# Compressed attention of a two-layer decoder trunk: two token blocks through one chain of small steps, the zeroing factor in the gates, and 8 KB of DMA scratch

## The chip, the cores and the metric

The kernel runs on one core of a Trainium2 chip. The metric is the device time of one execution in microseconds (us), lower is better. A core has a matrix engine (PE, with its weight loads listed apart as PEld), a vector engine (DVE), a scalar engine (ACT), a general engine (POOL) and a queue engine (SP) that only starts transfers. Each engine works through its own instructions in order, and the engines wait for one another through semaphores.

## The reference, cut to what matters

The program computes two decoder layers on 512 tokens of width 1024. Layer 0 holds the part that is changed: sparse attention with three branches, whose outputs are added with sigmoid gates. The first branch is the compressed one. Keys and values are compressed to 31 entries (one per 16 tokens, each covering 32), and each query attends to those that end at or before its own position:

```python
m_c = cmp_end[None, :] <= t[:, None]
p_c = masked_softmax(jnp.einsum('bgrqd,bgcd->bgrqc', q_b, k_c) * scale, m_c)
o_c = jnp.einsum('bgrqc,bgcd->bgrqd', p_c.astype(v_c.dtype), v_c)
o_c = jnp.where(m_c.any(-1)[:, None], o_c, 0)
...
return g_b[..., 0:1] * o_c + g_b[..., 1:2] * o_s + g_b[..., 2:3] * o_w
```

The `where` sets the result to zero for the first 31 tokens, which see no compressed entry at all. The other two branches (selected blocks and a window) are, at 512 tokens, both causal attention over all earlier tokens, with keys and values of their own.

There are 12 query heads in 3 groups of 4; a group shares its keys and values. Beside them layer 0 has attention over a memory of 256 entries. An output projection, a squared-ReLU MLP, and a second layer with its own attention and MLP follow.

## The kernel before, in words

**Stages.** The tokens lie in four blocks of 128. `setup` and the first part of `layer_a` compute the projection of group 0 and of the compressed branch (to about 60 us). Then comes the attention of layer 0 (to about 300 us), the output projection, the MLP of layer 0 (to about 660 us), layer B with its attention (to about 930 us) and the second MLP. The MLPs are long rows of matrix products.

**Items.** `attend` (L142) walks through a list of items. An item has a front (scores, maximum, exponential, scaling) and a back (transposes of the probabilities, their copy out of PSUM, and at the end of a half the product with the values). The back of an item is issued after the front of the next one. A *light* item of the two token branches covers a query block with at most 256 keys and takes one PSUM tile for its scores (L1050); a *heavy* one takes two (L1063). The order within a group is four light items, four heavy ones, and the same again for the second pair of heads.

**Compressed items.** `cmp_scores` (L969) builds the front and back of a compressed item, one per token block and group, 12 in all. The front is four small matrix products (L985) into a PSUM tile, then a chain: two DVE additions that read that tile (L990 with the mask, L991 with its second half), a DVE maximum (L993), a DVE subtraction (L994), an exponential on ACT (L995), a DVE sum (L997), a reciprocal (L998), a multiplication with the gate (L1003; for block 0 L1001, which also multiplies with `self.zc`, the column of zeros for the first 31 tokens), and a multiplication of the probabilities on POOL (L1004). The PSUM tile is free again when L991 has read it. The back is one transpose (L1009) and its copy into `pcT` by `evT` (L737): every third call goes to DVE (L741), the others to ACT (L743), counted by the running number `self.n`, which every new tile raises too. When the last block's back is done, `close` (L1037) runs the product with the compressed values (L1015, in `cmp_out`).

**PSUM tiles for scores.** Three banks serve all score tiles in turn (`ps`, L207, with `pS` and `px`), for the transposes there are two (`pT`).

**Where the items stand.** `spread` (L173) puts the compressed items between the others: in group 0 all four after the eighth item; in groups 1 and 2 one after each of the first four items (L841).

**Filler.** After every front and every back `tick` (L147) takes some steps from a list of other work: the projections of the next group (`proj_a`), of the memory queries (`mem_q`), the memory keys, and more. `RA` (L47) says how many steps per tick in each of the three groups and in the memory items. Two of these jobs start only when 20 items of a group have been issued (`seen.count(...) == 20`, L834 and L835). A second list, `slow`, starts one step of `blocks` (L1172) after every 13 ticks (`PA`): a transfer within device memory of 1 MB, four plain ones from ACT's queue (L1180) and then four that add, from POOL's queue (L1183), for each quarter of each MLP. The MLP goes on with them, eight per quarter (`PM`).

**Order.** The program is written in this order, but a planner in the framework orders each engine's instructions before the run from estimated durations, so an engine's row in the trace need not follow the source.

Of the kernel before, what the change touches and what calls it, by code (L numbers as in the profile page):

```python
# [11 lines left out]
ALU = mybir.AluOpType  # L12
AX = mybir.AxisListType

P = 128
D = 1024
S = 512
NB = 4
# [28 lines left out]
RA = (2.0, 1.16, 1.46, 1.96)  # L47
# [133 lines left out]
class K:  # L181
# [602 lines left out]
    def layer_a(self):  # L784
# [8 lines left out]
        def evac0(b, ps):  # L793
            t = self.t("x", [P, 384])
            nc.scalar.activation(t, ps[:, 0:384], AF.Copy, scale=st[0][:, b : b + 1])
            raw0.append(t)
            nc.scalar.activation(gt[:, b, :], ps[:, 384:420], AF.Copy, scale=st[0][:, b : b + 1])
            if b < NB - 1:
                return
            ga = ab[:, 0:144]  # L800
            nc.vector.tensor_scalar(out=ga, in0=ga, scalar1=-1.0, scalar2=80.0, op0=ALU.mult, op1=ALU.min)
            nc.scalar.activation(ga, ga, AF.Exp)
            nc.vector.tensor_scalar(out=ga, in0=ga, scalar1=1.0, scalar2=None, op0=ALU.add)
            nc.vector.reciprocal(out=ga, in_=ga)

# [28 lines left out]
        work.add(self.proj_a(2, xg, st, ga[2]), "g2", lambda: seen.count(0) == 20)  # L834
        work.add(self.mem_q(0, xg, ins["w_am"], e, qm), None, lambda: seen.count(1) == 20)  # L835
# [5 lines left out]
        items = spread(L[0], C[0], 8, 0) + spread(L[1], C[1], 1, 1) + spread(L[2], C[2], 1, 1) + M  # L841
# [127 lines left out]
    def cmp_scores(self, g, q4, cmp, gt):  # L969
# [12 lines left out]
        def front(i):  # L982
            Sc = self.ps(self.pS, [P, 4, 2, 32])
            for h in range(4):
                nc.tensor.matmul(  # L985
                    Sc[:, h].rearrange("p t c -> p (t c)"), q4[h // 2][:, h % 2, i * P : (i + 1) * P],
                    KC[:, g].rearrange("p t c -> p (t c)"), start=True, stop=True,
                )
            s = self.t("cs", [P, 4, 32])
            nc.vector.tensor_tensor(out=s, in0=Sc[:, :, 0], in1=bcast(self.ccm[:, i, :], 1, 4), op=ALU.add)  # L990
            nc.vector.tensor_tensor(out=s, in0=Sc[:, :, 1], in1=s, op=ALU.add)  # L991
            m = self.t("c1", [P, 4])
            nc.vector.tensor_reduce(out=m, in_=s, axis=AX.X, op=ALU.max)  # L993
            nc.vector.tensor_tensor(out=s, in0=s, in1=bcast(m, 2, 32), op=ALU.subtract)  # L994
            nc.scalar.activation(s, s, AF.Exp)  # L995
            z = self.t("c2", [P, 4])
            nc.vector.tensor_reduce(out=z, in_=s, axis=AX.X, op=ALU.add)  # L997
            nc.vector.reciprocal(out=z, in_=z)  # L998
            gc = gt[:, i, :].rearrange("p (h b) -> p h b", b=3)[:, 4 * g : 4 * g + 4, 0]
            if i == 0:  # L1000
                nc.vector.scalar_tensor_tensor(out=z, in0=z, scalar=self.zc, in1=gc, op0=ALU.mult, op1=ALU.mult)  # L1001
            else:
                nc.vector.tensor_tensor(out=z, in0=z, in1=gc, op=ALU.mult)  # L1003
            nc.gpsimd.tensor_tensor(out=s, in0=s, in1=bcast(z, 2, 32), op=ALU.mult)  # L1004
            return s

        def back(i, s):
            pt = self.ps(self.pT, [P, P])
            nc.tensor.transpose(pt, s.rearrange("p h c -> p (h c)"), self.idf)  # L1009
            self.evT(pcT[:, i * P : (i + 1) * P], pt)  # L1010
# [9 lines left out]
    def attn_a(self, g, ga, gt, cmp, out):  # L1020
# [60 lines left out]
        def back(pr, half, hp, ii, p):  # L1081
# [43 lines left out]
            [Item(cfront, cback, (i,), g, "cmp") for i in range(NB)],  # L1125
# [695 lines left out]
```

## Time and profile before

| what | us |
|---|---|
| median of 3 runs | 1273.14 |
| lowest, highest | 1271.8, 1274.15 |
| the profiled execution, its own time | 1268.89 |
| its span, first to last instruction | 1267.1 |

Busy time over that span: PE 1238.2, PEld 1019.6, DVE 835.9, ACT 750.7, POOL 343.1. The granted clock of the matrix engine was 0.998 over the span. A busy PE means that one of its matrix products is under way; products overlap, so a busy PE need not be at its peak rate.

The views that the next part uses are these. The page begins with the busy time of each engine. A table of stretches gives the busy time of each engine between two times. The list of waits says which engine stood still for whom, at which line. Groups of instructions by line give count, total busy time and mean duration; kept apart by shape they tell how the duration of an operation grows with its size. The timeline lists single instructions, with the idle time before them in square brackets and what ended it.

### The profile page before, as it was taken

Reading aid. Unit: us, or ns where it says so; the run is one execution under the profiler, and the core shown is the slowest. Engines: PE = TensorE matmul, PEld = TensorE weight load, DVE = VectorE, ACT = ScalarE, POOL = GpSimd, SP = SyncE. Lnnn points to the kernel's source line nnn. Section 1 sums busy time; section 2 is a strip of 40 time slices with the busy share of each in tenths; the row PEclk is TensorE's granted clock in tenths of the full one; section 3 lists DMA queues with packets and bytes.
Section 4 is the critical chain, followed back from the end, with each engine's and each line's share of the span. In section 5 each row is a group of like instructions: output and inputs, shape, how many; then the busy total and the mean of one; then the engine's idle time right before and its main releaser. Section 6 shows DMA issues by size and latency. Waiting matters only on the chain.

```text
span 1267.1 us, 18289 instructions
## 1 busy us (share of the span) xinstructions
PE 1238.2 (98%) x6416; PEld 1019.6 (80%) x6416; DVE 835.9 (66%) x1516; ACT 750.7 (59%) x1668; POOL 343.1 (27%) x448
## 2 busy tenths in 40 slices
PE   9999989899999999999999999999999999999998
PEld 7768777677788888888888898987788888888887
DVE  6846676755656557566579567787766756656566
ACT  6845578774575364453647457788666445364462
POOL 4546675632040010000002788552222000000000
PEclk9999999999999999999999999999999999999999
DMA  7531241335488697896976331210459789696534
GB/s 266 198 112 65 68 132 61 67 76 135 157 250 239 225 274 220 268 242 216 282 205 190 120 101 58 63 47 9 117 190 277 220 271 241 219 279 204 164 102 164
DMA packets 61835, 215.26 MB, mean 170 GB/s; under 512 B 6736, under 2 KB 14928, under 8 KB 61232
## 3 DMA queue, kind: packets, MB, share of 16 engines
q1 hardware_dynamic: 50656, 143.69, 34.2%
q0 software_dynamic: 9344, 35.77, 14.2%
q10 hardware_dynamic: 1744, 34.63, 7.6%
q8 instruction: 51, 0.84, 0.3%
q14 instruction: 40, 0.33, 0.1%
HBM read 208.83 MB, written 72.35 MB: 222 GB/s over the span
## 4 chain that ended last, share of the span: by engine, by line
PE 80%; DVE 7%; ACT 7%; POOL 2%; issue 2%; DMA 2%; ACTq 0%; POOLq 0%; DVEq 0%
PE s_ps L270 13%; PE s_ps L271 13%; PE s_ps L272 13%; PE s_acc L270 6%; PE s_acc L271 6%; PE s_acc L272 6%; PE s_po L747 3%; PE s_pt L270 3%; PE s_pt L272 3%; PE s_pt L271 3%; ACT s_p L226 1%; DVE s_w L265 1%; PE s_acc L880 1%; PE s_acc L579 1%; PE s_pt L1100 1%
## 5 line engine op out<-in xcount | busy, mean ns | idle before, releaser
L265 DVE TENSOR_TENSOR s_w<-s_st,s_w 128x1024 fp32r<-128x1024 f32 (+3 forms) x254 | 291.0, 1151 | 260.5 <-ACT s_w L263 250.8
L263 ACT ACTIVATE s_w<-s_st 128x1024 fp32r<-128x1024 f32 (+4 forms) x260 | 251.5, 970 | 182.4 <-PE s_pt L272 45.9
L270 PE MATMUL s_ps<-s_act,s_w 128*128 128x512 f32 x568 | 222.0, 393 | 1.1 <-ACT s_act L305 0.7
L271 PE MATMUL s_ps<-s_act,s_w 128*128 128x512 f32 x568 | 221.1, 390 | 0.0
L272 PE MATMUL s_ps<-s_act,s_w 128*128 128x512 f32 x568 | 221.0, 390 | 0.0
L270 PEld LDWEIGHTS s_ps<-s_act,s_w 128*128 128x128 f32 x568 | 106.5, 188 | 24.4 <-ACT s_act L305 1.6
L271 PEld LDWEIGHTS s_ps<-s_act,s_w 128*128 128x128 f32 x568 | 106.7, 188 | 22.9 <-issue 0.8
L272 PEld LDWEIGHTS s_ps<-s_act,s_w 128*128 128x128 f32 x568 | 106.6, 188 | 22.1
L226 ACT ACTIVATE s_p<-s_ps 128x512 f32<-128x512 f32 x64 | 38.2, 598 | 117.9 <-PE s_ps L272 117.1
L270 PE MATMUL s_acc<-s_w,s_act 128*128 128x512 f32 (+3 forms) x288 | 101.4, 357 | 2.3 <-ACT s_sq L518 1.5
L271 PE MATMUL s_acc<-s_w,s_act 128*128 128x512 f32 (+3 forms) x288 | 101.2, 354 | 0.2 <-DVE s_w L265 0.2
L272 PE MATMUL s_acc<-s_w,s_act 128*128 128x512 f32 (+3 forms) x288 | 100.4, 354 | 0.0
L1183 POOL DMA_DIRECT2D sum<-in_w_db_dram x16 | 14.4, 900 | 291.1 <-ACT s_p L226 287.5
L735 POOL TENSOR_SCALAR s_p<-s_p,s_cr,s_ab 128x128 f32<-128x128 f32 (+3 forms) x96 | 61.1, 673 | 55.3 <-DVE s_cr L1076 28.5
L226 ACT ACTIVATE s_p<-s_ps,s_nm 128x256 f32<-128x256 f32 (+3 forms) x128 | 65.6, 523 | 16.4 <-DVE s_nm L726 5.0
L270 PEld LDWEIGHTS s_acc<-s_w,s_act 128*128 128x128 f32 x288 | 54.7, 190 | 8.7 <-ACT s_sq L518 2.5
L743 ACT ACTIVATE s_pt<-s_pt 128x512 f32<-128x512 f32 (+2 forms) x101 | 53.0, 528 | 13.6 <-PE s_pt L1100 6.0
L305 ACT ACTIVATE s_qk<-s_p 128x256 fp32r<-128x256 f32 (+1 forms) x96 | 46.9, 489 | 21.1 <-DVE s_p L1193 19.2
L271 PEld LDWEIGHTS s_acc<-s_w,s_act 128*128 128x128 f32 x288 | 54.8, 190 | 4.7 <-DVE s_w L265 0.4
L272 PEld LDWEIGHTS s_acc<-s_w,s_act 128*128 128x128 f32 x288 | 54.7, 190 | 4.3
L1183 POOL DMA_DIRECT2D sum<-sum x16 | 14.1, 883 | 151.0 <-issue 39.2
L308 DVE TENSOR_TENSOR s_qk<-s_p,s_qk 128x256 fp32r<-128x256 f32 (+1 forms) x96 | 50.0, 520 | 0.7 <-ACT s_qk L305 0.6
(332 smaller groups left out, 2869.3 us busy)
## 6 DMA issues: line engine op xcount, KB each, us to landing
s_st<-in_w_up_dram SPq DMA_DIRECT2D x64, 512.0 KB, 4.3
s_st<-sum SPq DMA_DIRECT2D x64, 512.0 KB, 6.7
s_st<-in_w_db_dram SPq DMA_DIRECT2D x48, 512.0 KB, 4.5
sum<-in_w_db_dram POOLq DMA_DIRECT2D x16, 1024.0 KB, 14.1
sum<-sum POOLq DMA_DIRECT2D x16, 1024.0 KB, 11.0
s_st<-in_w_bq_dram SPq DMA_DIRECT2D x16, 384.0 KB, 3.1
s_st<-in_w_ag_dram SPq DMA_DIRECT2D x11, 512.0 KB, 3.4
s_w<-in_w_c_dram SPq DMA_DIRECT2D x8, 512.0 KB, 4.4
```

The source lines that it names most:

```text
L226: return lambda *a, **k: self.marks.append(f(*a, **k))
L263: nc.scalar.activation(w[:, 0], st, AF.Copy)
L265: e.tensor_tensor(out=w[:, 1], in0=st, in1=w[:, 0], op=ALU.subtract)
L270: mm(ps, lh[0], rh[0], start=start, stop=False, skip_group_check=again)
L271: mm(ps, lh[0], rh[1], start=False, stop=False, skip_group_check=again)
L272: mm(ps, lh[1], rh[0], start=False, stop=stop, skip_group_check=again)
L305: nc.scalar.activation(dst[:, 0], src, AF.Copy)
L308: nc.vector.tensor_tensor(out=dst[:, 1], in0=src, in1=dst[:, 0], op=ALU.subtract)
L735: self.nc.gpsimd.tensor_scalar(out=p, in0=p, scalar1=c, scalar2=g, op0=ALU.mult, op1=ALU.mult)
L743: self.turned = self.nc.scalar.activation(dst, src, AF.Copy)
L747: i = self.nc.tensor.matmul(*a, **k)
L1183: self.behind(self.nc.gpsimd.dma_start(t[o], x, accum_op=ALU.add, max_dma_last_dim=4096))
```

## The change

A compressed item now takes two token blocks. Its front issues eight matrix products into one PSUM tile of twice the size (one full bank), and every step of the chain works on both blocks at once; its back issues two transposes into one tile, with one copy. There are two items per group, six in all. The factor `zc` is multiplied into the gates of block 0 once, for all 12 heads, in `evac0`, right after the gates have been computed. `RA` is raised in the first three entries in the ratio of the item counts (20 to 18 items per group), the conditions on the item count go from 20 to 18, and in groups 1 and 2 the compressed items stand after the first and the third of the other items (`every` is 2 in place of 1). The scratch for transfers issued by software, a parameter of the program, is set to 8192 bytes.

```diff
-RA = (2.0, 1.16, 1.46, 1.96)
+RA = (2.22, 1.29, 1.62, 1.96)
...
             nc.vector.reciprocal(out=ga, in_=ga)
+            g0 = gt[:, 0, :].rearrange("p (h k) -> p h k", k=3)[:, :, 0]
+            nc.vector.tensor_scalar(out=g0, in0=g0, scalar1=self.zc, scalar2=None, op0=ALU.mult)
...
-        work.add(self.proj_a(2, xg, st, ga[2]), "g2", lambda: seen.count(0) == 20)
-        work.add(self.mem_q(0, xg, ins["w_am"], e, qm), None, lambda: seen.count(1) == 20)
+        work.add(self.proj_a(2, xg, st, ga[2]), "g2", lambda: seen.count(0) == 18)
+        work.add(self.mem_q(0, xg, ins["w_am"], e, qm), None, lambda: seen.count(1) == 18)
...
-        items = spread(L[0], C[0], 8, 0) + spread(L[1], C[1], 1, 1) + spread(L[2], C[2], 1, 1) + M
+        items = spread(L[0], C[0], 8, 0) + spread(L[1], C[1], 1, 2) + spread(L[2], C[2], 1, 2) + M
...
-            Sc = self.ps(self.pS, [P, 4, 2, 32])
-            for h in range(4):
...
+            Sc = self.ps(self.pS, [P, 2, 4, 2, 32])
+            for b in range(2):
+                blk = slice((2 * i + b) * P, (2 * i + b + 1) * P)
+                for h in range(4):
...
-            nc.vector.tensor_tensor(out=s, in0=Sc[:, :, 0], in1=bcast(self.ccm[:, i, :], 1, 4), op=ALU.add)
-            nc.vector.tensor_tensor(out=s, in0=Sc[:, :, 1], in1=s, op=ALU.add)
-            m = self.t("c1", [P, 4])
+            s = self.t("cs", [P, 2, 4, 32])
+            nc.vector.tensor_tensor(out=s, in0=Sc[:, :, :, 0], in1=bcast(self.ccm[:, 2 * i : 2 * i + 2], 2, 4), op=ALU.add)
+            nc.vector.tensor_tensor(out=s, in0=Sc[:, :, :, 1], in1=s, op=ALU.add)
+            m = self.t("c1", [P, 2, 4])
             nc.vector.tensor_reduce(out=m, in_=s, axis=AX.X, op=ALU.max)
...
-            if i == 0:
-                nc.vector.scalar_tensor_tensor(out=z, in0=z, scalar=self.zc, in1=gc, op0=ALU.mult, op1=ALU.mult)
-            else:
-                nc.vector.tensor_tensor(out=z, in0=z, in1=gc, op=ALU.mult)
-            nc.gpsimd.tensor_tensor(out=s, in0=s, in1=bcast(z, 2, 32), op=ALU.mult)
+            nc.vector.tensor_tensor(out=z, in0=z, in1=gc, op=ALU.mult)
+            nc.gpsimd.tensor_tensor(out=s, in0=s, in1=bcast(z, 3, 32), op=ALU.mult)
             return s

         def back(i, s):
-            pt = self.ps(self.pT, [P, P])
-            nc.tensor.transpose(pt, s.rearrange("p h c -> p (h c)"), self.idf)
-            self.evT(pcT[:, i * P : (i + 1) * P], pt)
+            pt = self.ps(self.pT, [P, 2, P])
+            for b in range(2):
+                nc.tensor.transpose(pt[:, b], s[:, b].rearrange("p h c -> p (h c)"), self.idf)
+            self.evT(pcT[:, 2 * i * P : (2 * i + 2) * P].rearrange("p (b q) -> p b q", b=2), pt)
...
-            if i == NB - 1:
+            if i == NB // 2 - 1:
...
-            [Item(cfront, cback, (i,), g, "cmp") for i in range(NB)],
+            [Item(cfront, cback, (i,), g, "cmp") for i in range(NB // 2)],
...
-    nc = bacc.Bacc("TRN2", target_bir_lowering=False, num_devices=1)
+    nc = bacc.Bacc("TRN2", target_bir_lowering=False, num_devices=1, dynamic_dma_scratch_size=8192)
```

More of the change, by code (lines that the diff above doesn't have):

```diff
@@ L982, in front @@
         def front(i):
-            Sc = self.ps(self.pS, [P, 4, 2, 32])
-            for h in range(4):
[L985 to L991, printed above, removed]
@@ L992, in front @@
-            m = self.t("c1", [P, 4])
+            Sc = self.ps(self.pS, [P, 2, 4, 2, 32])
+            for b in range(2):
+                blk = slice((2 * i + b) * P, (2 * i + b + 1) * P)
+                for h in range(4):
+                    nc.tensor.matmul(
+                        Sc[:, b, h].rearrange("p t c -> p (t c)"), q4[h // 2][:, h % 2, blk],
+                        KC[:, g].rearrange("p t c -> p (t c)"), start=True, stop=True,
+                    )
+            s = self.t("cs", [P, 2, 4, 32])
@@ L993, in front @@
+            nc.vector.tensor_tensor(out=s, in0=Sc[:, :, :, 0], in1=bcast(self.ccm[:, 2 * i : 2 * i + 2], 2, 4), op=ALU.add)
+            nc.vector.tensor_tensor(out=s, in0=Sc[:, :, :, 1], in1=s, op=ALU.add)
+            m = self.t("c1", [P, 2, 4])
             nc.vector.tensor_reduce(out=m, in_=s, axis=AX.X, op=ALU.max)
-            nc.vector.tensor_tensor(out=s, in0=s, in1=bcast(m, 2, 32), op=ALU.subtract)
+            nc.vector.tensor_tensor(out=s, in0=s, in1=bcast(m, 3, 32), op=ALU.subtract)
@@ L995, in front @@
             nc.scalar.activation(s, s, AF.Exp)
-            z = self.t("c2", [P, 4])
+            z = self.t("c2", [P, 2, 4])
             nc.vector.tensor_reduce(out=z, in_=s, axis=AX.X, op=ALU.add)
             nc.vector.reciprocal(out=z, in_=z)
-            gc = gt[:, i, :].rearrange("p (h b) -> p h b", b=3)[:, 4 * g : 4 * g + 4, 0]
-            if i == 0:
-                nc.vector.scalar_tensor_tensor(out=z, in0=z, scalar=self.zc, in1=gc, op0=ALU.mult, op1=ALU.mult)
-            else:
-                nc.vector.tensor_tensor(out=z, in0=z, in1=gc, op=ALU.mult)
@@ L1004, in front @@
-            nc.gpsimd.tensor_tensor(out=s, in0=s, in1=bcast(z, 2, 32), op=ALU.mult)
+            gc = gt[:, 2 * i : 2 * i + 2, :].rearrange("p b (h k) -> p b h k", k=3)[:, :, 4 * g : 4 * g + 4, 0]
+            nc.vector.tensor_tensor(out=z, in0=z, in1=gc, op=ALU.mult)
+            nc.gpsimd.tensor_tensor(out=s, in0=s, in1=bcast(z, 3, 32), op=ALU.mult)
             return s
         def back(i, s):
-            pt = self.ps(self.pT, [P, P])
-            nc.tensor.transpose(pt, s.rearrange("p h c -> p (h c)"), self.idf)
```

## The prediction

> **What bounds the kernel now.** I read the busy times of the page first, then busy time by stretch, then the list of waits of the matrix engine in the stretches that hold compressed items, then the timeline there.
>
> ```profile
> PE 1238.2 (98%) x6416; PEld 1019.6 (80%) x6416; DVE 835.9 (66%) x1516; ACT 750.7 (59%) x1668; POOL 343.1 (27%) x448
> ```
>
> PE is busy in all but 28.9 of 1267.1 us. The change removes no matrix product and no transpose: 48 products of L985 and 12 transposes of L1009 stay. So it can only win where PE stands still, and the question is how much of its idle time belongs to the compressed items. The next view is the table of stretches (length, busy time and instructions of each engine). The first two hold the compressed items of groups 1 and 2 from the first product of L985 to the last transpose of L1009; the other three are what lies before, between and behind.
>
> ```profile
> core 0: us, PE busy (x) PEld busy (x) DVE busy (x) ACT busy (x) POOL busy (x), PEclk, DMA share, GB/s
> 168.00:191.00 23.00, 19.81 (x145) 16.09 (x146) 19.30 (x55) 17.64 (x58) 14.48 (x21) 1.00 0.43 139
> 222.00:245.00 23.00, 19.52 (x148) 15.17 (x149) 17.32 (x56) 16.38 (x58) 13.48 (x24) 1.00 0.37 64
> 150.00:168.00 18.00, 16.55 (x107) 13.14 (x105) 13.27 (x27) 13.81 (x36) 14.02 (x17) 1.00 0.20 59
> 191.00:222.00 31.00, 28.54 (x220) 22.98 (x219) 21.06 (x52) 25.82 (x80) 17.04 (x25) 1.00 0.19 60
> 245.00:281.00 36.00, 33.84 (x213) 26.48 (x213) 20.89 (x49) 27.90 (x83) 15.24 (x23) 1.00 0.36 85
> ```
>
> In the first two PE is idle 3.19 + 3.48 = 6.67 of 46 us; in the neighbours 1.45 + 2.46 + 2.16 = 6.07 of 85 us, which is 0.071 per us. At that rate 46 us would have 3.28 us of idle, so 3.39 us are in excess. The engine that differs is DVE: busy 36.62 of 46 us (0.796) with compressed items, 55.22 of 85 (0.650) without. ACT is not busier there (0.740 against 0.795). The waits of PE in the same two stretches (total, times, longest), the three largest of each:
>
> ```profile
> PE s_ps L1065 <- ACT s_p L226: 1.0, 1, 1.0
> PE s_ps L1052 <- DVE s_cs L991: 0.8, 1, 0.8
> PE s_ps L1065 <- DVE s_cs L991: 0.7, 2, 0.4
> ...
> PE s_pt L1100 <- DVE s_pt L741: 1.3, 1, 1.3
> PE s_ps L1065 <- ACT s_p L226: 1.1, 2, 0.9
> PE s_pt L1009 <- ACT s_pt L743: 0.8, 1, 0.8
> ```
>
> PE waits for a score bank that L991 has not yet read (1.5 us), or that an exponential (L226) has not, which itself comes behind a DVE maximum. The 1.3 us go back to the chain too, as the DVE timeline shows:
>
> ```profile
> 226.15 1.43 DVE L994 TENSOR_TENSOR s_cs<-s_cs,s_c 128x128 f32<-128x128 f32 x1
> 227.51 0.54 DVE L741 COPY s_pt<-s_pt 128x384 f32<-128x384 f32 x1
> ...
> 225.50 2.78 POOL L735 TENSOR_SCALAR s_p<-s_p,s_cr,s_ab 128x512 f32<-128x512 f32 x4
> ```
>
> (The last row is POOL's.) The copy that PE waited for stood behind a subtraction of the chain that took 1.43 us. So in these stretches the bound is DVE's queue, and the chain is what fills it.
>
> **The chain, before and after.** These are the chain's groups between 60 and 300 us (count | busy us, mean ns | idle before).
>
> ```profile
> L990 DVE TENSOR_TENSOR s_cs<-s_ps,c 128x128 f32<-128x128 f32 x12 | 3.3, 277 | 2.6 <-PE s_pt L1009 2.0 <-PE s_ps L985 0.5
> L991 DVE TENSOR_TENSOR s_cs<-s_ps,s_cs 128x128 f32<-128x128 f32 x12 | 3.4, 284 | 0.1
> L993 DVE TENSOR_REDUCE s_c<-s_cs 128x4 f32<-128x128 f32 x12 | 3.4, 280 | 0.1
> L994 DVE TENSOR_TENSOR s_cs<-s_cs,s_c 128x128 f32<-128x128 f32 x12 | 4.8, 400 | 0.1
> L997 DVE TENSOR_REDUCE s_c<-s_cs 128x4 f32<-128x128 f32 x12 | 3.3, 277 | 1.1 <-ACT s_cs L995 1.1
> L998 DVE RECIPROCAL s_c<-s_c 128x4 f32<-128x4 f32 x12 | 2.0, 170 | 0.1
> L1001 DVE SCALAR_TENSOR_TENSOR s_c<-s_c,c,s_ab 128x4 f32<-128x4 f32 x3 | 2.3, 780 | 0.0
> L1003 DVE TENSOR_TENSOR s_c<-s_c,s_ab 128x4 f32<-128x4 f32 x9 | 2.8, 309 | 0.2
> L995 ACT ACTIVATE s_cs<-s_cs 128x128 f32<-128x128 f32 x12 | 3.7, 310 | 3.1 <-DVE s_cs L994 3.0
> L1004 POOL TENSOR_TENSOR s_cs<-s_cs,s_c 128x128 f32<-128x128 f32 x12 | 4.8, 400 | 3.0 <-DVE s_c L1003 2.4 <-PE s_ps L1066 0.4 <-DVE s_c L1001 0.2
> ```
>
> DVE spends 25.3 us on 84 instructions. For the doubled size I take other lines that work on 128x256 in the same stretch:
>
> ```profile
> L958 DVE TENSOR_TENSOR s_tq<-s_acc,gr 128x256 f32<-128x256 f32 x8 | 3.3, 418 | 0.7 <-ACT s_x L955 0.6
> L520 DVE TENSOR_REDUCE s_r<-s_sq 128x4 f32<-128x256 f32 x8 | 3.3, 413 | 5.0 <-ACT s_sq L518 5.0
> L711 DVE TENSOR_TENSOR s_qki<-s_tq,s_qki 128x256 fp32r<-128x256 f32 x6 | 3.2, 528 | 0.7 <-ACT s_qki L710 0.5
> L518 ACT ACTIVATE s_sq<-s_acc 128x256 f32<-128x256 f32 x8 | 3.1, 385 | 0.0
> L743 ACT ACTIVATE s_pt<-s_pt 128x256 f32<-128x256 f32 x8 | 3.1, 383 | 0.3 <-PE s_pt L1094 0.3
> L759 POOL TENSOR_TENSOR s_tq<-s_tq,s_r 128x256 f32<-128x256 f32 x4 | 2.5, 618 | 1.2 <-DVE s_r L527 1.2
> L743 ACT ACTIVATE s_x<-s_pt 128x128 f32<-128x128 f32 x8 | 2.2, 276 | 1.9 <-PE s_pt L1009 1.9
> ```
>
> - **DVE:** a pair costs 2 x 0.418 (L990, L991) + 2 x 0.413 (L993, L997) + 0.528 (L994, both inputs in SBUF like L711) + 0.170 + 0.309 = 2.67 us, six pairs 16.0 us. Saved: 9.3 us, or 0.775 per block; for the 8 blocks of the two stretches 6.2 us.
> - **ACT and POOL:** six exponentials of 0.385 in place of 12 of 0.310 save 1.4 us; a copy of 0.383 replaces two of 0.276; six multiplications of 0.618 in place of 12 of 0.400 save 1.1 us. None is the bound; I put these at nothing.
> - **From DVE to PE:** DVE's share falls from 0.796 to (36.62 - 6.2) / 46 = 0.661, which is 0.92 of the way to the neighbours. I take the same part of the excess: 0.92 x 3.39 = 3.1 us. The upper end is all 3.39, or, if the idle time of both stretches went entirely, 6.67. The lower end: only the waits that name the chain or its copies (0.8 + 0.7 + 1.3 + 0.8 = 3.6) come half as often, 1.8 us.
> - **Group 0:** its four blocks lie beside the projection of group 1, and no large wait of PE names them. Nothing; had that filler run out, DVE's 3.1 us there would count too, as a gain.
>
> L994 is blocked, not slow: other instructions of its size take a fifth of its 1.43 us, and POOL was reading SBUF meanwhile (the four scalings of L735 shown above). On this the Trainium skill, SBUF — State Buffer, section Who interferes with whom, says that a DVE instruction with two SBUF inputs and a GpSimd instruction that reads SBUF exclude each other. By that rule half the instructions meet half the collisions, as the means above have it; if collisions grew with the elements instead, DVE would save less, and the gain would lie nearer its lower end.
>
> **The factor in the gates.** One DVE instruction more, on 48 columns, behind the reciprocal of the gates. The nearest row:
>
> ```profile
> L801 DVE TENSOR_SCALAR s_ab<-s_ab x1: 235/235/235, 52.8 to 52.8; 128x144 f32<-128x144 f32 x1
> ```
>
> I charge 0.2 us in full, since PE waits shortly there; the bounds are 0 and 0.235.
>
> **Order and filler.** Per group the ticks give 40 x 2.0 = 80 steps before and 36 x 2.22 = 79.9 after, 46.4 and 46.4, 58.4 and 58.3: the same filler, with its weight loads on SP. In groups 1 and 2 two light items now lie between the compressed ones, and none stands right ahead of the first heavy item. At nothing: PE-bound filler covers it.
>
> **Transfers within device memory.** The items fall from 68 to 62, the ticks from 136 to 124. The 12th item is out after 22 ticks, so 114 become 102, and with one start in 13 ticks after the first 13, eight starts become seven. The eighth, an adding one on POOL, moves into the first eighth of the MLP.
>
> ```profile
> L1183 POOL DMA_DIRECT2D sum<-sum x16: 872/880/923, 253.5 to 1146.4; - x16
> ...
> DMA to landing us min/median/max: 7.7/13.2/17.5
> ```
>
> It takes POOL 0.88 us and lands within 17.5; its sum is needed only in the third product after eight up-projections, each of 24 matrix products. At nothing; if that cover were gone, 13.2 us would show. The scratch of 8 KB also costs nothing in my sum: no issue in the row above stretches (923 ns at most). From the other side, one issue held until an earlier transfer lands would hold POOL's queue, and the scalings of L735 in it, for 13.2 us.
>
> **Sum.** -3.1 + 0.2 = -2.9 us. Against the profiled execution 1268.89 gives 1266.0. The median of the runs shown is 4.25 us above that execution; I carry the difference over: 1273.1 - 2.9 = **1270.2 us**.
>
> **Rivals.**
>
> *A, only the named waits shrink.* The largest single wait in both stretches has ACT's exponential behind it, and ACT is as busy as before. If freeing DVE doesn't move these, the gain is 1.8 - 0.2 = 1.6 us: 1271.5. For it: the 2.1 us of L226. Against it: the maxima that precede these exponentials stand in DVE's queue.
>
> *B, slower: the bank is held longer.* A pair keeps its score bank from its first product until L991 has read both blocks, and PE's next scores wait in order behind that.
>
> ```profile
> 168.73 0.63 PE L985 MATMUL s_ps<-KC,s_qk 128*128 128x64 f32 x4
> 105.99 0.86 PE L985 MATMUL s_ps<-KC,s_qk 128*128 128x64 f32 x7
> 183.34 0.27 PE L1009 MATMUL s_pt<-c,s_cs 128*128 128x128 f32 x1
> ```
>
> Eight products take some 0.95 us for 0.63, the two additions 0.84 for 0.56: 0.60 us more per pair. It decides once PE reaches the next scores before L991 has ended; that was so at 3 of 8 blocks, 0.5 us each. Were it so at all four pairs, PE would lose 4 x 1.1 = 4.4 in place of 1.5 us: +2.9 + 0.2 = +3.1, 1276.2. Against it: the bank falls due half as often, and no longer right ahead of a heavy item. The longer chain itself holds nobody: the first transpose of group 1 came 14.6 us after its scores. The Trainium skill speaks for B: Perfetto Trace Analysis, section Optimizing Scalar/DVE Operations, advises breaking instructions up where an engine that isn't saturated causes bubbles on another; DVE is such an engine here, and the change does the opposite.
>
> *C, the stage is planned anew.* The idle 6.07 us of the neighbours hangs on an order that the planner now makes again, with other items side by side and copies falling otherwise to DVE or ACT. Half of it more or less is 3 us: with the forecast's gain 1267.2 to 1273.2, with none of it up to 1276.
>
> *D, the scratch.* One held issue: POOL 13.2 us late, of which I estimate 10 reach PE beyond the 3 of filler, minus the gain: about 1280. Against it stand the even durations of L1183.
>
> **How the numbers follow.** Chances: forecast (gains of 1.5 to 4.5 us) 0.42, A 0.22, B 0.12, C 0.22, D 0.02. A measurement can tell about 0.2% (2.5 us) from no change. Faster by more: 0.33 of the forecast's 0.42 and 0.09 of C, 0.42. Within: 0.09 of the forecast, A whole, 0.07 of C, 0.38. Slower: B, D, 0.06 of C, 0.20. The range reaches from the whole idle time of both stretches saved (1273.1 - 6.6 = 1266.5) to a little past B (1276.5).
>
> **What would show it.** Right: L990 to L998 with 6 instructions each and about 16 us of DVE in all; DVE's share in the stretches with compressed items near 0.66; PE's idle time there near 0.08 per us; waits on L991 at most half. Wrong: waits on L991 of 1 us each (B); unchanged waits on L226 (A); idle time moved into the neighbours (C); an L1183 far above 0.9 us (D). The forecast falls if PE's idle time doesn't follow DVE's share.

## The result and the profile after

| | before, us | after, us |
|---|---|---|
| median (range, runs), run side by side | 1272.77 (1271.8 to 1274.15, 4) | 1262.41 (1261.71 to 1263.52, 4) |
| profiled execution, its span | 1268.89, 1267.1 | 1263.52, 1261.6 |
| the same pair once more, later | 1271.2 (median of 13) | 1262.2 (1260.37 to 1265.19, 4) |

The ratio after/before is 0.9919 with an interval of 0.9901 to 0.9936, and 0.993 (0.9907 to 0.9954) the second time: 9 to 10 us faster. The forecast was 1270.2 us with a range from 1266.5, so the direction was right and the size was not: 2.9 us were forecast.

The page of the kernel after begins:

```profile
PE 1236.7 (98%) x6416; PEld 1019.9 (81%) x6416; DVE 831.0 (66%) x1477; ACT 748.3 (59%) x1654; POOL 335.8 (27%) x442
```

DVE lost 39 instructions and 4.9 us, and PE has as many instructions as before. The span is 5.5 us shorter with 1.5 us less of PE's busy time, so 4.0 us of PE's idle time went. Where, the table of stretches of the kernel after tells (the columns as in the prediction):

```profile
100.00:168.00 68.00, 66.54 (x395) 55.06 (x392) 46.56 (x104) 44.76 (x125) 42.70 (x54) 1.00 0.23 72
168.00:191.00 23.00, 20.82 (x146) 16.95 (x145) 16.70 (x42) 17.32 (x55) 16.53 (x24) 0.94 0.28 93
191.00:222.00 31.00, 29.21 (x233) 24.34 (x232) 19.93 (x52) 25.46 (x82) 14.97 (x22) 0.99 0.29 94
222.00:245.00 23.00, 21.68 (x163) 17.32 (x162) 17.90 (x47) 18.05 (x61) 15.56 (x25) 1.00 0.26 47
245.00:281.00 36.00, 35.12 (x219) 27.80 (x218) 21.45 (x50) 26.96 (x83) 13.82 (x23) 1.00 0.35 79
```

From 168 to 281 us PE is idle 2.18 + 1.79 + 1.32 + 0.88 = 6.17 us; before it was 3.19 + 2.46 + 3.48 + 2.16 = 11.29. Of the 5.1 us, 3.2 come from the two stretches that held the compressed items, 2.0 from their neighbours. DVE's share in the two is (16.70 + 17.90) / 46 = 0.75, not the 0.66 that was forecast. By an estimate the chain takes 5.4 us less there (two thirds of 25.3 before, two thirds of 17.2 after, the sums of its lines), and since DVE is busy only 2.0 us less, some 3.4 us of other work came into the same time.

How far the work has come is read from the first and last start of a line. The columns are count, duration in ns (least, median, most), first and last start in us, and shape. The kernel before, with the last product with the compressed values and then the first transpose of the MLP:

```profile
L1015 PE MATMUL s_po<-s_x,s_vcb x12: 592/618/697, 149.5 to 301.0; 128*128 128x512 f32 x12
...
L1231 PE MATMUL s_pt<-c,s_x x64: 270/272/273, 332.1 to 951.4; 128*128 128x128 f32 x64
```

The kernel after (its lines stand two further down):

```profile
L1017 PE MATMUL s_po<-s_x,s_vcb x12: 592/594/697, 145.1 to 293.2; 128*128 128x512 f32 x12
...
L1233 PE MATMUL s_pt<-c,s_x x64: 270/272/276, 327.3 to 946.0; 128*128 128x128 f32 x64
```

The last compressed product starts 7.8 us earlier, the MLP 4.8, its last transpose 5.4. So the whole gain is made before the MLP. Between the two points lie 31.1 us before and 34.1 after, 3.0 us more (rival C, below, says with which part of the change they come), and nothing more happens behind them.

### The profile page after: what moved, and what is told of

Read it like the earlier page. It is cut to its first block, busy times and chain, and to the rows that moved or that the text cites. A ratio compares the mean times of both kernels' runs of the same rounds, so it can differ in the third digit from the quotient of the medians.

```text
span 1261.6 us, 18237 instructions
## 1 busy us (share of the span) xinstructions
PE 1236.7 (98%) x6416; PEld 1019.9 (81%) x6416; DVE 831.0 (66%) x1477; ACT 748.3 (59%) x1654; POOL 335.8 (27%) x442
## 4 chain that ended last, share of the span: by engine, by line
PE 70%; DVE 6%; ACT 5%; DMA 4%; issue 2%; POOL 1%; ACTq 0%; POOLq 0%; DVEq 0%
PE s_ps L270 13%; PE s_ps L271 13%; PE s_ps L272 13%; PE s_acc L270 4%; PE s_acc L272 4%; PE s_acc L271 4%; PE s_pt L270 3%; PE s_pt L272 3%; PE s_pt L271 3%; PE s_po L747 3%; DMA s_st<-in_w_ao_dram 2%; DVE s_w L265 1%; ACT s_p L226 1%; ACT s_w L263 1%; PE s_ps L1558 1%
## 5 line engine op out<-in xcount | busy, mean ns | idle before, releaser
L226 ACT ACTIVATE s_p<-s_ps 128x512 f32<-128x512 f32 x64 | 38.1, 595 | 93.5 <-PE s_ps L272 92.0
L226 ACT ACTIVATE s_p<-s_ps,s_nm 128x256 f32<-128x256 f32 (+3 forms) x128 | 65.4, 523 | 9.9 <-DVE s_nm L726 4.3
L743 ACT ACTIVATE s_pt<-s_pt 128x512 f32<-128x512 f32 (+2 forms) x97 | 50.5, 523 | 17.2 <-PE s_pt L1102 9.5
L271 PE MATMUL s_acc<-s_w,s_qk 128*128 128x512 f32 x128 | 49.9, 390 | 0.0
```

Source lines behind the costliest of these rows:

```text
L226: return lambda *a, **k: self.marks.append(f(*a, **k))
L271: mm(ps, lh[0], rh[1], start=False, stop=False, skip_group_check=again)
L743: self.turned = self.nc.scalar.activation(dst, src, AF.Copy)
```

## The experiments

The expectations number the theories in the order in which they were formed and say what each holds. The theory that remained is the last: *a score bank was held because the chain's tile `cs` has two buffers.* In each experiment the median with its range and number of runs, and the ratio to runs of the kernel before on the same chip with its interval, are given. The kernel before and the kernel after each ran again as they are; these two give the scale.

**e4, e5: both kernels again.** No edit.

> The kernel before, unchanged, for a second profiled execution. Its first profiled execution took 1268.89 us where the timed runs took 1271.8 to 1274.15. If that execution was an exception, this one takes 1271 to 1275 us and its trace shows some 3 to 5 us more idle time of PE in the attention of layer 0, which the first trace hid; if a profiled execution is always faster than a timed one, it is again near 1269 us.

> The changed kernel, unchanged, as the measure for the three runs beside it. Before it, its four runs gave 1261.7 to 1263.5 us, and e1 (steps per block) 1261.9 to 1265.3. Theory 1, reduced: merging the steps is worth about 2 us of the gain, so this run lies 1 to 3 us below e1: 1261 to 1263.5 us. Theory 2 (all of it is order and tiles): the same as e1, 1263 to 1265.

Before: 1270.95 (1268.11 to 1274.09, 10), ratio 1.0 (0.9988 to 1.0011). After: 1262.2, as in the table above. The profiled execution of e4 took 1271.91, 3.0 us more than the first profile of the same kernel. Part of that is PE's clock, as the stretches of e4 show (the granted clock is the third number from the end):

```profile
191.00:222.00 31.00, 28.64 (x208) 23.26 (x209) 19.88 (x52) 24.82 (x77) 16.71 (x24) 0.94 0.19 60
222.00:245.00 23.00, 19.72 (x143) 15.70 (x140) 16.89 (x54) 15.01 (x54) 12.95 (x22) 0.93 0.31 53
```

It was 0.94 and 0.93 there, where the first profile has 1.00. The 3 to 5 us of additional idle time that the expectation named are not there: from 100 to 310 us PE is idle 12.6 us in e4 and 13.2 in the first profile. The first profile of before was a quick execution; by e4's, the change gained 8.4 us.

**e1: the chain's steps undone.** The kernel after with each step of the chain done per block on 128x128 again; one bank, one transpose tile, one copy and six items stay.

```diff
-            nc.vector.tensor_tensor(out=s, in0=Sc[:, :, :, 0], in1=bcast(self.ccm[:, 2 * i : 2 * i + 2], 2, 4), op=ALU.add)
+            for b in range(2):
+                j = 2 * i + b
+                nc.vector.tensor_tensor(out=s[:, b], in0=Sc[:, b, :, 0], in1=bcast(self.ccm[:, j, :], 1, 4), op=ALU.add)
...
```

> The changed kernel with its items, their places, its tiles, its one copy per pair and its filler as they are, but each step of the chain (the seven on DVE, the exponential on ACT, the multiplication on POOL) issued once per block, 128x128 each, as before the change. Theory 1 (fewer and larger instructions free DVE's queue, and PE waits less): the chain's DVE time goes from 17 back to about 23 us or more, and most of the gain is lost: 1268 to 1273 us. Theory 2 (the gain comes from the order: half as many items, placed otherwise, and a plan made anew): most of the gain stays: 1262 to 1265 us.

1264.21 (1261.88 to 1265.27, 4); 0.9947 (0.9929 to 0.9964). Nearly the whole gain is there without the merged steps. They may be worth the 2 us between this and e5, but the intervals overlap. The table of stretches of e1, 100 to 310 us:

```profile
100.00:310.00 210.00, 200.88 (x1299) 160.93 (x1297) 140.41 (x360) 144.28 (x438) 110.00 (x164) 1.00 0.29 81
```

Next to it, the same stretch of before and of after:

```profile
100.00:310.00 210.00, 196.79 (x1275) 158.13 (x1274) 143.50 (x355) 142.19 (x432) 114.14 (x161) 1.00 0.31 85
```

```profile
100.00:310.00 210.00, 202.36 (x1309) 163.40 (x1307) 134.90 (x318) 143.86 (x432) 109.14 (x158) 0.99 0.29 83
```

DVE is busy 140.41 us, near before's 143.50, and PE is busy 200.88, near after's 202.36. A smaller DVE load was not what PE had lacked.

**e3, e11: the scratch and the gates alone.** The kernel before with 8 KB of scratch, and the kernel before with the factor in the gates.

```diff
-    nc = bacc.Bacc("TRN2", target_bir_lowering=False, num_devices=1)
+    nc = bacc.Bacc("TRN2", target_bir_lowering=False, num_devices=1, dynamic_dma_scratch_size=8192)
```

> The kernel before with the scratch for transfers at 8192 bytes and nothing else. Theories 1 and 2: no difference, 1271 to 1275 us. Theory 3 (the scratch or the tiles' new places in SBUF make the transfers or the engines faster): 1262 to 1268 us.

```diff
+            nc.vector.tensor_scalar(out=g0, in0=g0, scalar1=self.zc, scalar2=None, op0=ALU.mult)
...
-            if i == 0:
-                nc.vector.scalar_tensor_tensor(out=z, in0=z, scalar=self.zc, in1=gc, op0=ALU.mult, op1=ALU.mult)
-            else:
-                nc.vector.tensor_tensor(out=z, in0=z, in1=gc, op=ALU.mult)
+            nc.vector.tensor_tensor(out=z, in0=z, in1=gc, op=ALU.mult)
```

> The kernel before with only the zeroing factor multiplied into the gates (one DVE instruction of 48 columns more, and three chains with a plain product in place of one with the factor). By its instructions worth under 0.5 us. If the time moves by 2 us or more, a nearly neutral edit is enough to make the planned order better or worse by that much, and differences of such a size between the other runs say nothing on their own; if it stays at 1270 to 1272 us, they do.

e3: 1270.22 (1269.0 to 1273.44, 10); 1.0002 (0.999 to 1.0015). e11: 1269.56 (1268.27 to 1271.36, 10); 0.9993 (0.9984 to 1.0003). Neither moves the time by anything that can be measured. e11 also says that a small edit that makes the planner lay out the order anew need not bring several microseconds; that another place of items can cost as much, e2 shows below.

**e7, e8, e12: places and filler as before.** The kernel after with compressed items after each of the first two others (e7), with the old `RA` (e8), with both (e12).

```diff
-        items = spread(L[0], C[0], 8, 0) + spread(L[1], C[1], 1, 2) + spread(L[2], C[2], 1, 2) + M
+        items = spread(L[0], C[0], 8, 0) + spread(L[1], C[1], 1, 1) + spread(L[2], C[2], 1, 1) + M
```

> The changed kernel, but in groups 1 and 2 its two pairs stand after the first and the second light item (a distance of 1, as before the change) instead of the first and the third. If the places carry the gain (2b): 1266 to 1271 us. If the tiles do (2a): within 2 us of the changed kernel.

```diff
-RA = (2.22, 1.29, 1.62, 1.96)
+RA = (2.0, 1.16, 1.46, 1.96)
```

> The changed kernel, but with the filler's rate per tick of the kernel before (2.0, 1.16, 1.46), so that about a tenth of the filler (8 of 80, 5 of 46, 6 of 58 steps) moves behind its group. If denser filler between the items carries the gain: 1266 to 1272 us. If not: within 2 us of the changed kernel.

> The changed kernel with both the filler's rate of the kernel before (as in e8, 1260.5 us) and the old distance of the pairs (as in e7, 1262.3 us). If e8's gain over the changed kernel is the rate's and not chance, 1259 to 1261.5 us; if it was chance of the planned order, 1262 us or more.

e7: 1262.31 (1261.94 to 1263.35, 4); 0.993 (0.9911 to 0.9949). e8: 1260.53 (1260.26 to 1261.6, 4); 0.9914 (0.9892 to 0.9936). e12: 1262.44 (1261.12 to 1263.31, 4); 0.9936 (0.9914 to 0.9957). All three are the kernel after within their intervals. e8 is the lowest median of the study, but e12, with the same `RA`, does not repeat it.

**e6, e10: the shared PSUM tiles undone.** The kernel after with the scores of a pair in two banks (e6; the two additions that read them then work per block), and with two transpose tiles and two copies (e10).

```diff
-            Sc = self.ps(self.pS, [P, 2, 4, 2, 32])
+            s = self.t("cs", [P, 2, 4, 32])
+            Scs = []
             for b in range(2):
+                Sc = self.ps(self.pS, [P, 4, 2, 32])
+                Scs.append(Sc)
...
```

> The changed kernel, but the scores of a pair go into two score tiles, one bank per block, so that the compressed items take 12 turns of the three score banks instead of 6; L994 and L995 work per block (128x128), every other step on both blocks. Theory 2a (the gain comes from fewer turns of the score banks, on which PE waits for a reader): the gain falls by half or more, 1266 to 1271 us. Theory 2b (it comes from fewer and differently placed items and the order made from them): 1262 to 1265 us.

```diff
-            pt = self.ps(self.pT, [P, 2, P])
             for b in range(2):
-                nc.tensor.transpose(pt[:, b], s[:, b].rearrange("p h c -> p (h c)"), self.idf)
-            self.evT(pcT[:, 2 * i * P : (2 * i + 2) * P].rearrange("p (b q) -> p b q", b=2), pt)
+                pt = self.ps(self.pT, [P, P])
+                nc.tensor.transpose(pt, s[:, b].rearrange("p h c -> p (h c)"), self.idf)
+                self.evT(pcT[:, (2 * i + b) * P : (2 * i + b + 1) * P], pt)
```

> The changed kernel, but the two transposes of a pair go into two tiles with a copy each, so that the compressed items take 12 turns of the two transpose banks instead of 6, and 12 copies out of PSUM instead of 6. If the transpose banks or copies carry a part of the gain: 1264 to 1268 us. Theory 2a with score banks alone: within 1.5 us of the changed kernel, 1261 to 1263.5 us.

e6: 1267.93 (1267.11 to 1270.09, 10); 0.9973 (0.9962 to 0.9985). It loses 5.7 us against e5, more than half of the gain, as theory 2a (the turns of the score banks) expected. e10: 1265.43 (1264.74 to 1267.99, 10); 0.9965 (0.9954 to 0.9976), 3.2 us lost. So both kinds of shared PSUM tile matter; which matters more isn't shown, since the two intervals overlap.

**e2, e9: pairs without a shared chain.** The kernel before with 12 items, where in groups 1 and 2 two neighbours stand together (e2), and in all groups with one bank for both (e9). The chain stays as it was.

```diff
+def pairs(a, b):
+    a = list(a)
+    return a[:1] + list(b[:2]) + a[1:3] + list(b[2:]) + a[3:]
...
-        items = spread(L[0], C[0], 8, 0) + spread(L[1], C[1], 1, 1) + spread(L[2], C[2], 1, 1) + M
+        items = spread(L[0], C[0], 8, 0) + pairs(L[1], C[1]) + pairs(L[2], C[2]) + M
```

> The kernel before, with its 12 compressed items of one block, but in groups 1 and 2 two of them next to each other, after the first and the third light item, which is where the change puts its pairs. Theory 1: the chain costs DVE what it did, so 1270 to 1275 us. Theory 2 (order): a good part of the gain shows, 1262 to 1267 us.

```diff
-            Sc = self.ps(self.pS, [P, 4, 2, 32])
...
+            if i % 2 == 0:
+                S2[0] = self.ps(self.pS, [P, 2, 4, 2, 32])
...
+            Sc = S2[0][:, i % 2]
```

> As e2 (the kernel before with 12 compressed items, two next to each other in groups 1 and 2; 1276.6 us), but the two blocks of a neighbouring pair share one score tile: the first item's front issues all eight products into one bank, the second item's front only its chain. The steps stay per block, 128x128 each, two transposes with two tiles and two copies. Theory 2a (turns of the score banks, 12 to 6): 5 us or more below e2, 1267 to 1272 us. Theory 2b (the number of items and what is woven between them): near e2, 1274 to 1279 us.

e2: 1276.63 (1275.19 to 1279.73, 5); 1.005 (1.0032 to 1.0068). e9: 1275.92 (1273.82 to 1278.28, 5); 1.0044 (1.0028 to 1.0061). Both are *slower* than before, and e2 lies above what either theory expected: moving items, with nothing else, cost 6 us. The theory that half as many turns of a bank are the whole gain falls with e9: it has them and loses 5 us. It doesn't follow that turns cost nothing; e6 shows that in the kernel after they do.

**What the timeline showed then.** Since the waits that name the chain were small, I measured for each score tile how long it is in use, from its first product (L985) to the end of the second addition (L991). In group 0 of before, on PE (start in us, duration, count of products in the row):

```profile
107.92 0.64 PE L985 MATMUL s_ps<-KC,s_qk 128*128 128x64 f32 x5
110.15 0.61 PE L985 MATMUL s_ps<-KC,s_qk 128*128 128x64 f32 x4
...
129.38 0.27 PE L1009 MATMUL s_pt<-c,s_cs 128*128 128x128 f32 x1
140.34 0.27 PE L1009 MATMUL s_pt<-c,s_cs 128*128 128x128 f32 x1
```

and on DVE:

```profile
131.06 0.27 DVE L990 TENSOR_TENSOR s_cs<-s_ps,c 128x128 f32<-128x128 f32 x1
131.37 0.29 DVE L991 TENSOR_TENSOR s_cs<-s_ps,s_cs 128x128 f32<-128x128 f32 x1
140.86 0.28 DVE L990 TENSOR_TENSOR s_cs<-s_ps,c 128x128 f32<-128x128 f32 x1
141.18 0.29 DVE L991 TENSOR_TENSOR s_cs<-s_ps,s_cs 128x128 f32<-128x128 f32 x1
```

The scores of the third and fourth block are there at 108.6 and 110.8 us, and nobody reads them until 131 and 141: each addition starts within 1.5 us of the end of a transpose. L990 writes a `cs` tile, `cs` has two buffers, and a buffer comes free when its transpose (L1009) has read it. Blocks 1 and 2 hold both, so blocks 3 and 4 hold two of the three score banks for 24 and 31 us. In group 0 DVE has other work meanwhile. The view of line L990 of before says whom DVE stood still for ahead of it, over the whole run (us, times; the 2.0 us lie in group 2, ahead of the addition at 235 us):

```profile
  PE s_pt L1009: 2.0, 1
  PE s_ps L985: 0.5, 1
```

An addition that reads scores and waits for a *transpose* must wait for the place that it writes to: by the source it takes nothing else from the transposed tile. In the kernel after a `cs` buffer holds two blocks, so two buffers hold all four, and the first addition of the second pair no longer waits for a transpose. The timeline of after, DVE, the second pair of group 0 (first and last row are PE's):

```profile
107.35 1.42 PE L989 MATMUL s_ps<-KC,s_qk 128*128 128x64 f32 x12
...
109.12 0.41 DVE L994 TENSOR_TENSOR s_cs<-s_ps,c 128x256 f32<-128x256 f32 x1
110.24 0.41 DVE L995 TENSOR_TENSOR s_cs<-s_ps,s_cs 128x256 f32<-128x256 f32 x1
...
134.71 0.38 PE L1011 MATMUL s_pt<-c,s_cs 128*128 128x128 f32 x2
```

Its scores are read within 3 us, and the transposes come 24 us behind and hold nobody. That gave four experiments.

**e13, e16: more buffers, no pair.** The kernel before with four buffers (e13) or three (e16) of `cs` and of its two small tiles, and with the 8 KB of scratch, which makes the room.

```diff
-        ... r7=2, nm=6, su=5, cr=6, c1=2, c2=2, nb=4,
-        cs=2, stt=4, vcb=1, ab=1,
+        ... r7=2, nm=6, su=5, cr=6, c1=4, c2=4, nb=4,
+        cs=4, stt=4, vcb=1, ab=1,
```

> The kernel before with four buffers in place of two for the tiles of the compressed chain (cs, c1, c2), and the scratch at 8192 bytes to make the room; 12 items, single steps, all else as before. In the trace of before the third block's first addition (L990) starts only after the first block's transpose (L1009) has freed its cs buffer, and until then the third and the fourth block hold two of the three score banks, for 24 and 31 us in group 0 and 7 to 12 us in groups 1 and 2. Theory 4 (the gain comes from these held banks: a pair needs two cs buffers for four blocks): most of the gain appears without any pair, 1262 to 1266 us. Theories 2a and 2b (bank turns, items): 1269 to 1272 us.

> The kernel before with three buffers for cs, c1 and c2 (before: two; e13: four, 1265.5 us) and the scratch at 8192 bytes. Only the fourth block of a group must now wait for the first block's transpose, so one of the three score banks is held in place of two. Theory 4: a time between the two, 1266.5 to 1269 us, with the fourth block's bank alone held for more than 6 us. If it is as fast as e13, a held bank costs only where two are held; if as slow as before, one held bank is enough.

e13: 1265.47 (1264.57 to 1267.81, 10); 0.9963 (0.9954 to 0.9973). With no pair at all it is 4.5 us faster than the 24 runs of before beside it. e16: 1270.03 (1267.85 to 1274.84, 10); 0.9996 (0.9983 to 1.001), no gain, where the theory of held banks expected 1266.5 to 1269. But its profile (1270.21 us, near its median) has a stop that no score tile causes. On ACT (first row) and PE, between group 1, whose last compressed transpose starts at 198 us, and group 2, whose first scores start at 226:

```profile
209.38 1.06 ACT L263 ACTIVATE s_w<-s_st 128x1024 fp32r<-128x1024 f32 x1 [1.44 <-DMA s_st<-in_w_mem_dram]
...
211.07 0.63 PE L1100 MATMUL s_pt<-c,s_p 128*128 128x128 f32 x4 [2.59 <-ACT s_pt L743]
```

The copy that PE waits for stands behind a scaling of weights, which waited for a transfer. PE's longest stop between the groups is 1.2 us in before and 1.4 in e13. From 191 to 222 us the granted clock is also 0.94 here and 1.00 in those two. So e16 doesn't say what one held bank costs.

**e14, e15: the same from the other side.** The kernel after with one `cs` buffer, and e9 with four.

```diff
-        cs=2, stt=4, vcb=1, ab=1,
+        cs=1, stt=4, vcb=1, ab=1,
```

> The changed kernel with one cs buffer in place of two, so that the second pair of a group waits in its score bank until the first pair has been transposed, as the third block did before. Theory 4: most of the gain is lost, 1267 to 1273 us. Without theory 4: within 2 us of the changed kernel, 1261 to 1264 us.

> As e9 (12 items, two next to each other in groups 1 and 2, one score bank for both, 1275.9 us), with four buffers for cs, c1 and c2 and the scratch at 8192 bytes. Its banks were held for 34, 15 and 12 us by the second pair of each group. Theory 4: these holds fall below 6 us and the time by 6 us or more, to 1264 to 1270 us. Without theory 4: 1274 to 1278 us.

e14: 1269.85 (1267.06 to 1271.36, 10); 0.9988 (0.9976 to 0.9999): nearly the whole gain is lost, though every merged step is there. e15: 1270.18 (1268.22 to 1271.47, 10); 0.9997 (0.9987 to 1.0006), 5.7 us below e9, a little less than the 6 expected. The timeline of e14 shows the wait come back, for the second pair of group 0 (the square bracket is idle time of DVE and what ended it):

```profile
107.50 1.42 PE L989 MATMUL s_ps<-KC,s_qk 128*128 128x64 f32 x12
...
133.82 0.38 PE L1011 MATMUL s_pt<-c,s_cs 128*128 128x128 f32 x2
134.24 0.42 DVE L994 TENSOR_TENSOR s_cs<-s_ps,c 128x256 f32<-128x256 f32 x1 [1.77 <-PE s_pt L1011]
134.69 0.42 DVE L995 TENSOR_TENSOR s_cs<-s_ps,s_cs 128x256 f32<-128x256 f32 x1
```

How long the score tiles were in use, worked out from the timelines in the same way for all groups:

| kernel | longest of groups 0, 1, 2, us | sum of all tiles, us | median time, us |
|---|---|---|---|
| before (two buffers) | 31.3, 11.8, 9.6 | 106.3 | 1269.93 (24 runs beside e13) |
| e16, three buffers | 21.9, 8.5, 6.0 | 56.9 | 1270.03 |
| e13, four buffers | 5.6, 2.8, 3.4 | 30.4 | 1265.47 |
| e9, pairs share a bank | 34.0, 15.0, 12.2 | 69.9 | 1275.92 |
| e15, e9 with four buffers | 4.5, 5.8, 4.2 | 24.8 | 1270.18 |
| e14, after with one buffer | 27.3, 13.1, 10.8 | 60.1 | 1269.85 |
| after | 3.5, 4.8, 3.2 | 18.5 | 1262.2 (e5) |
| e1, after with single steps | 4.9, 5.6, 5.1 | 26.4 | 1264.21 |
| e10, after with two transpose tiles | 3.5, 4.4, 2.5 | 19.2 | 1265.43 |
| e6, after with two score banks | 2.9, 5.2, 2.4 | 28.2 | 1267.93 |

Where only buffers differ, beside the scratch, which alone does nothing (before and e13, e9 and e15, e14 and after), the time drops by 4.5 to 7.7 us where no tile is held beyond 6 us. It isn't the only thing that counts: no tile of e10 or e6 is held that long, and both are slower than after. The stretch from 100 to 310 us says it by engines. e13, then e14:

```profile
100.00:310.00 210.00, 199.90 (x1291) 160.09 (x1289) 141.54 (x359) 143.71 (x436) 114.06 (x161) 1.00 0.31 88
```

```profile
100.00:310.00 210.00, 196.16 (x1275) 158.70 (x1273) 134.64 (x312) 139.39 (x423) 109.26 (x156) 0.99 0.28 79
```

e14 has DVE's load of after (134.64 against 134.90) and PE's of before (196.16 against 196.79). e13 has a DVE load near before's and gets 3.1 us more out of PE. Here the time follows the number of `cs` buffers, not DVE's load.

## Why the prediction was wrong

**The bound (the step that failed).** "So in these stretches the bound is DVE's queue" was read from DVE's share of 0.80 beside 0.65 in the neighbours. But the runs show that the two need not go together. e1, with the steps of before, shows it best:

```profile
168.00:191.00 23.00, 20.57 (x152) 16.74 (x150) 19.61 (x59) 17.52 (x57) 17.26 (x27) 1.00 0.28 92
222.00:245.00 23.00, 22.23 (x163) 17.44 (x162) 18.20 (x61) 17.65 (x62) 15.31 (x26) 1.00 0.30 61
```

DVE is busy 37.81 of 46 us (0.82), more than before, and PE is idle 3.20 us in place of 6.67. From 168 to 191 us e13 has a larger DVE share than before or after (20.95 of 23 us) and less PE idle time than before; e14 has the smallest share of before, after, e13 and e14 from 222 to 245 and the most idle time. (In e13 from 222 to 245 both fell.) The rows of e13 and of e14:

```profile
168.00:191.00 23.00, 21.15 (x155) 17.18 (x154) 20.95 (x61) 18.79 (x62) 16.61 (x25) 1.00 0.40 138
```

```profile
222.00:245.00 23.00, 18.56 (x139) 15.04 (x135) 16.14 (x45) 14.61 (x52) 14.16 (x23) 0.99 0.39 92
```

PE is idle 1.85 us in the first (before 3.19) and 4.44 in the second (before 3.48). "The forecast falls if PE's idle time doesn't follow DVE's share": it does not. What the runs showed in its place: without any lighter load on DVE, four buffers of `cs` for two bring 4.5 us (e13), and one for two takes 7.6 of after's gain (e14). As I read it, PE lacked tiles for scores, held behind `cs`. The row that points there stood in the prediction, as the releaser of L990: 2.0 us of idle time of DVE until "PE s_pt L1009". I priced that line's duration and passed over its wait. The other trace of it was read the wrong way round: "The longer chain itself holds nobody: the first transpose of group 1 came 14.6 us after its scores." Until that transpose the first block keeps its `cs` buffer, and the third block's scores stay in their bank for 8.5 us.

**The waits that were put down to ACT.** The largest wait of PE, for a score bank that an exponential (L226) still reads, was seen as ACT's slowness, and rival A hung on it. (A calls it the largest single wait in both stretches; in the second the 1.3 us for a copy by DVE are larger.) With more buffers its sum falls. The waits of PE from 100 to 310 us (total, times, longest), first before, then after, e13, e14, e16 and e10:

```profile
PE s_ps L1065 <- ACT s_p L226: 4.0, 7, 1.2
```

```profile
PE s_ps L1067 <- ACT s_p L226: 1.9, 7, 0.4
```

```profile
PE s_ps L1065 <- ACT s_p L226: 1.7, 7, 0.3
```

```profile
PE s_ps L1067 <- ACT s_p L226: 4.5, 8, 1.3
```

```profile
PE s_ps L1065 <- ACT s_p L226: 3.6, 10, 0.8
```

```profile
PE s_ps L1067 <- ACT s_p L226: 3.4, 8, 0.9
```

The last row doesn't fit: e10 has after's buffers and no tile held beyond 4.4 us. Nor does one of the waits of before, 1.2 us at 208.6 us, when no compressed scores are in any bank.

For the others I read it so: while compressed scores sit in one or two banks, the light and heavy items have only the others, and a wait names the last reader of the bank that comes next in turn, not the tile that blocks the rest. No run shows it by itself. By it, A had the right wait with the wrong reason.

**The chain's terms.** The sizes held in the main. The chain in after, 60 to 300 us (count | busy us, mean ns | idle before):

```profile
L994 DVE TENSOR_TENSOR s_cs<-s_ps,c 128x256 f32<-128x256 f32 x6 | 2.5, 415 | 0.7 <-PE s_ps L989 0.6
L995 DVE TENSOR_TENSOR s_cs<-s_ps,s_cs 128x256 f32<-128x256 f32 x6 | 2.5, 412 | 0.0
L997 DVE TENSOR_REDUCE s_c<-s_cs 128x8 f32<-128x256 f32 x6 | 2.4, 408 | 0.0
L998 DVE TENSOR_TENSOR s_cs<-s_cs,s_c 128x256 f32<-128x256 f32 x6 | 4.0, 674 | 0.0
L1001 DVE TENSOR_REDUCE s_c<-s_cs 128x8 f32<-128x256 f32 x6 | 2.5, 411 | 0.5 <-ACT s_cs L999 0.5
L1002 DVE RECIPROCAL s_c<-s_c 128x8 f32<-128x8 f32 x6 | 1.1, 191 | 0.0
L1004 DVE TENSOR_TENSOR s_c<-s_c,s_ab 128x8 f32<-128x8 f32 x6 | 2.2, 369 | 0.1
```

DVE spends 17.2 us on it, against 16.0 forecast; the subtraction was taken too short (528 ns for 674). Beyond the additions beside it it takes 262 ns now (674 - 412) and took 123 before (400 - 277), so six cost as much extra time as twelve did; the prediction had taken the collisions with POOL to halve with the instructions. The first addition no longer has a transpose among its releasers, and the sign "waits on L991 at most half" came true: after has no wait of PE on L995 from 100 to 310 us. e13, with the old chain, keeps 0.9 us on L991 and 1.3 us on the copy behind the subtraction of 1.43 us. So the waits that the forecast named are real, and they may be a part of what after has beyond e13. But the step *from DVE to PE* ("0.92 x 3.39 = 3.1 us") multiplied a right term with a wrong cause. PE's idle time in the two stretches did fall to (2.18 + 1.32) / 46 = 0.076 per us, as forecast. That agreement is not the forecast's mechanism: DVE's share stayed at 0.75, and the neighbours, which were the yardstick, lost 2.0 us of idle time too. That is also why the range was too narrow: its lower end, the whole idle time of the two stretches, put every gain outside them at nothing.

**Group 0 at nothing.** Its banks were held longest, and yet PE's idle time from 100 to 168 us only fell from 1.91 to 1.46 us (1.76 in e13): the filler lies beside it. That the filler covers it was right. So the length of a hold alone doesn't say what it costs.

**Gates, scratch, order.** At nothing within what can be measured: e11, e3, e7 and e12. Rival D falls; the adding transfers of after are issued as before:

```profile
L1185 POOL DMA_DIRECT2D sum<-sum x16: 869/878/972, 277.0 to 1182.6; - x16
```

What the scratch does is make room for the larger `cs` tiles, in after as in e13.

**Rival B, the slower one.** It looked at the right thing, how long a bank is held, with the sign turned: the pair does not hold it longer. It is in use for 2.0 to 4.8 us, where the first two blocks of before took 1.4 to 3.4 and the others 7.5 to 31.3. B was priced from the first two kinds of row alone. The sentence of the Trainium skill in Perfetto Trace Analysis, section Optimizing Scalar/DVE Operations, to break instructions up where an unsaturated engine causes bubbles on another, finds no support here: e1 breaks them up again and is not faster than after (0.9947 beside 0.993). Nor is it refuted, since DVE's load is not what made the bubbles.

**Rival C.** What came back between the last compressed product and the MLP (31.1 to 34.1 us) looked like it. It is not in e13, whose two points lie 31.2 us apart as before's do:

```profile
L1015 PE MATMUL s_po<-s_x,s_vcb x12: 590/594/697, 149.7 to 297.3; 128*128 128x512 f32 x12
...
L1231 PE MATMUL s_pt<-c,s_x x64: 270/272/273, 328.5 to 947.5; 128*128 128x128 f32 x64
```

It comes with the raised `RA`: the distance is 33.0 to 35.4 us in after, e1, e5, e6, e7, e10 and e14, which have the new `RA`, and 30.2 and 30.1 in e8 and e12, the kernel after with the old one. There the last compressed product starts later (295.4 and 297.0 us, 293.2 in after) and the MLP about when it does in after (325.6 and 327.1, 327.3). So, as I read it, other work lies on the other side of the point, and no gain was lost there.

**The median's offset.** The forecast lies 7.8 us above the result, and its base is a part of that. 1273.1 was the median of three runs, and the later medians of before, of 13 to 24 runs, are 1269.9 to 1271.2: some 2 to 3 us come from the base, the other 5 to 6 from the gain, which was forecast as 2.9. Against the profiled executions the miss looks like 2.5 us (1266.0 forecast, 1263.52 measured), but only because the first profile of before was a quick execution. Carrying its distance of 4.25 us over was wrong too: after's median (1262.41) lies 1.1 us below its profiled execution, not above.

**What stays open.** That the buffers of `cs` cost time is shown from both sides. That they do so through the banks is argued, not shown. For it: e6, which takes one more bank per pair, loses 5.7 us, so a further turn of a score bank costs something. But e6 loses them without any long hold, more buffers also let the chain itself run earlier, and no run parts the two; e16 is no clean reading of one held bank. Every edit also makes the planner order the work anew, and e2 shows that another order alone can cost 6 us. Against chance speaks that the buffers move the time the same way from three different kernels: e13 shows 4.5 us for them, e9 and e15 5.7, e14 7.6 in the other direction. The kernel after gains some 3 us more than e13, and these were not taken apart cleanly: the merged steps (e1, 2 us, intervals overlapping), the shared bank (e6) and the shared transpose tile (e10) each cost when undone, and their sum is larger than the rest that they should explain. Why pairs cost some 5 us with the old chain in e15 as well (e15 against e13, 4.7 us) wasn't tried further.

## What to carry to other kernels

Where a tile in PSUM is read by a step that writes to a small tile with few buffers, the buffers of the *small* tile can decide how long the PSUM bank is held; measure from a tile's first product to its last read, for every tile, before believing the list of waits. The list of waits may not name the tile that is held at all: here its largest entry named the readers of other tiles. An engine's larger share in the stretches where PE stands still is no cause until a second reading, such as its releasers, agrees.

## What the runs showed that was not expected

- Three buffers (e16) took away half of the holding time (106.3 to 56.9 us) and gave no gain; four gave 4.5 us. That one held bank costs as much as two doesn't follow, because of the stop of 2.59 us in e16's profile.
- The subtraction with both inputs in SBUF took 674 ns on 128x256, the additions that read PSUM 412 to 415.
- Runs of an unchanged kernel spread over 6 us (1268.1 to 1274.1 in e4). The granted clock of a stretch is one part of it: 1.00 and 1.00 in the first profile of before, 0.94 and 0.93 in e4, from 191 to 245 us.
